# S5 scan: factors and one product of each step held in a PSUM bank

## The chip, the cores and the metric

The kernel runs on one core of a Trainium2 chip. The metric is the device time of one execution in microseconds; the time before is the median of three runs.

## The reference, cut to what matters

The model is a two-layer hybrid: layer 0 mixes an SSD block and an S5 block, layer 1 is attention. 256 context tokens and 2048 latent tokens make 2304 positions. The change lies in the S5 block, whose recurrence is, per group g (32 groups), state p (64 states) and direction (two):

```python
step = jnp.exp(log_step)[:, None]
mag = jnp.exp(lr * step)
ab_re, ab_im = mag * jnp.cos(li * step), mag * jnp.sin(li * step)   # the constant factor, complex
# h[t] = ab * h[t-1] + bu[t], complex, as real and imaginary parts
_, _, h_re, h_im = lax.associative_scan(_complex_affine_combine, (a_re, a_im, bu_re, bu_im), axis=1)
y = einsum('btgp,gip->btgi', h_re, c_re) - einsum('btgp,gip->btgi', h_im, c_im)
```

All of it is float32, and the output is compared in float32.

## The kernel before

The program is one launch that goes through its stages in order: modulation and projections of layer 0, SSD, S5, the output of layer 0 with the projections of layer 1, attention. In the S5 stage (`s5`, from line 1114) a chunk is 16 positions, so there are NK = 144 chunks. Each partition holds one of 64 states of one of two directions (forward on partitions 0 to 63, backward on 64 to 127). V is a tile of 128 x 145 x 2 x 32: chunk, real or imaginary part, group.

The S5 stage has three parts. The first (`front_u`, `front_b`, `chunk_inputs`, up to line 1206) fills V[:, 1:] with what each chunk adds to the state. The second (lines 1305 to 1323) is the scan over chunks, 143 steps, each of four VectorE instructions on 64 columns: line 1308 multiplies the state by the real factor A1 into t0, line 1309 multiplies the state with its two parts exchanged by A2 (the imaginary factor, minus and plus) into t1, line 1310 adds the next chunk's input to t0, and line 1311 adds t1 and writes the new state into V. A1 and A2 are two parts of the tile RT that came in by DMA. The third (`states`, `outputs`, `back`) copies V into tiles H (lines 1336 to 1338) and forms the outputs on TensorE.

The order of the work is written out by hand (`manual_schedule`): each engine runs its instructions in the order in which the code issues them, and waits at an instruction for what it needs from others. The loop of the scan also issues work for the other engines:

- `tables(q)` at steps 0, 16, ..., 112: six GpSimd tensor_tensor instructions on 128 x 1088, through `ctable` (lines 1137 to 1145). They depend on nothing in the scan.
- `tables_mm(q - 1)` at the same steps from 16 on, the last one behind the scan: eight TensorE products (line 1293), four ScalarE evictions (line 1294) and six DMAs to the table E in DRAM.
- `load_tt` (line 1251) and `own_chunk` every seventh step from 39: the part of the output inside a chunk, on TensorE (line 1257) and ScalarE (line 1265), into tile uT.
- every seventh step one step of the late modulation (`modulation`, lines 65 to 117): in this order a VectorE store `col` (line 104) of the job three steps back, a TensorE transpose `modt` (line 99) of the job two steps back, a ScalarE copy `modr` (line 90), and the products of a new job (lines 85 and 86), then the fetch of the weights two jobs ahead on SyncE (lines 78 and 80). `modt` has one buffer, so a transpose waits for the store of the transpose before. Only jobs 4 to 11 have a transpose and a store; the stores come with steps 49, 56, ..., 98.

PSUM in this stage: pool `s5ps` has three tags with two banks each, pool `s5m` one bank for `modt`.

Of the kernel before, what the change touches and what calls it, by code (L numbers as in the profile page):

```python
# [9 lines left out]
F32 = mybir.dt.float32  # L10
# [4 lines left out]
ALU = mybir.AluOpType  # L15
# [4 lines left out]
P = 128  # L20
# [99 lines left out]
def late_modulation(E, pool, wps, bank):  # L120

    return modulation(E, [(0, 2 * DM, 3 * DM, None), (1, 0, 3 * DM, E.col1)], 256, pool, wps, bank=bank)
# [851 lines left out]
NG = 32  # L974
# [47 lines left out]
def s5_views(t, parts=S5R):  # L1022

    R, o = {}, 0
    for n, w in parts:
        f = t[:, o:o + w]
        R[n] = f.rearrange("p (g j) -> p g j", j=16) if n in ("bbr", "bbi", "cr", "nci") else f.rearrange("p (n g) -> p n g", g=NG)
        o += w
    return R
# [84 lines left out]
def s5(E, finish, slots):  # L1114
# [4 lines left out]
    v, gp = nc.vector, nc.gpsimd  # L1119
    with ExitStack() as ctx:  # L1120
        pp = ctx.enter_context(tc.tile_pool(name="s5par", bufs=1, reuse_waits="tile"))
        RT = pp.tile([P, sum(w for _, w in S5R[2:])], F32, tag="RT", name="RT")
        R = s5_views(RT, S5R[2:])
        uT = pp.tile([P, NG, 2, NK], F32, tag="s5uT", name="s5uT")
        V = pp.tile([P, NK + 1, 2, NG], F32, tag="s5V", name="s5V")
        ctx.enter_context(tc.manual_schedule())

        def ctable(pr, pi, xr, xi, n, conj, o_r, o_i, tile_, engines):

            shp = [P, 4, n, 16]
            t, t2 = [tile_(i, shp) for i in range(2)]
            pw = lambda a: a.rearrange("p n g -> p g n").unsqueeze(3).to_broadcast(shp)
            xv = lambda a: a.unsqueeze(2).to_broadcast(shp)
            er, ei, g = engines
            g.tensor_tensor(out=t, in0=pw(pi), in1=xv(xi), op=ALU.mult)
            er.tensor_tensor(out=o_r, in0=pw(pr), in1=xv(xr), op=ALU.mult)
            g.tensor_tensor(out=t2, in0=pw(pi), in1=xv(xr), op=ALU.mult)
            yield  # L1140
            er.tensor_tensor(out=o_r, in0=o_r, in1=t, op=ALU.add if conj else ALU.subtract)
            yield
            ei.tensor_tensor(out=o_i, in0=pw(pr), in1=xv(xi), op=ALU.mult)
            yield
            ei.tensor_tensor(out=o_i, in0=o_i, in1=t2, op=ALU.subtract if conj else ALU.add)
# [100 lines left out]
        def load_tt(g, tt=None):  # L1246
            if tt is None:
                tt = ty.tile([P, 2, 256], F32, tag="tt", name="tt")
            ea = S["E"][g]
            for sb in range(2):  # L1250
                nc.sync.dma_start(out=tt[:, sb], in_=bass.AP(ea.tensor, ea.offset + P * sb, [[16, 8], [ESZ, 16], [1, 256]]))
            TT[g] = tt
# [6 lines left out]
        def own_chunk(g):  # L1259

            py = ps.tile([P, 2, NK], F32, tag="pu", name="py")
            for tb in range(2):
                within(g, py, tb)
            del TT[g]
            nc.scalar.activation(out=uT[:, g], in_=py, func=AF.Copy)
# [5 lines left out]
        with tc.tile_pool(name="s5s", bufs=2, reuse_waits="tile") as ss:  # L1271
            L48 = [ty.tile([P, 4, 48], F32, tag="L" + n, name="L" + n, bufs=1) for n in ("bbr", "bbi")]
            for t in L48:
                gp.memset(t, 0.0)

            def inputs(q):
                for n, t in zip(("bbr", "bbi"), L48):
                    for a, o in ((F, 0), (B, 16), (slice(0, P), 32)):
                        nc.scalar.activation(out=t[a, :, o:o + 16], in_=R[n][a, 4 * q:4 * q + 4], func=AF.Copy)

            def tables(q):
                sl = slice(4 * q, 4 * q + 4)
                for _ in ctable(R["PCr"][:, :, sl], R["PCi"][:, :, sl], R["cr"][:, sl], R["nci"][:, sl], 17, True, *CT[q],
                                lambda i, s: ss.tile(s, F32, tag=f"ct{i}", name="ct", bufs=1), (gp, gp, gp)):
                    pass

            def tables_mm(q):
                for g in (0, 2):
                    Q = ss.tile([48, 2, 272], F32, tag="Q", name="Q", bufs=2)
                    for gl in range(2):  # L1290
                        pq = ps.tile([48, 272], F32, tag="pv", name="pq")
                        for ri in range(2):
                            nc.tensor.matmul(pq, L48[ri][:, g + gl], fl(CT[q][ri][:, g + gl], 0, 17), start=(ri == 0), stop=(ri == 1))
                        nc.scalar.activation(out=Q[:, gl], in_=pq, func=AF.Copy)
                    dst = S["E"][4 * q + g:4 * q + g + 2].rearrange("g j e -> j g e")
                    nc.sync.dma_start(out=dst[:, :, 0:240], in_=Q[0:16, :, 16:256])
                    nc.sync.dma_start(out=dst[:, :, 256:496], in_=Q[16:32, :, 0:240])
                    nc.sync.dma_start(out=dst[:, :, 240:256], in_=Q[32:48, :, 256:272])
                if q < 7:
                    inputs(q + 1)  # L1300

            mps = ctx.enter_context(tc.tile_pool(name="s5m", bufs=2, space=PSUM, reuse_waits="tile"))
            mods = late_modulation(E, ss, mps, lambda: ps.tile([P, 512], F32, tag="pb", name="modps"))
            inputs(0)
            for i in range(NK - 1):
                t0 = ss.tile([P, 2, NG], F32, tag="t0", name="t0")
                t1 = ss.tile([P, 2, NG], F32, tag="t1", name="t1")
                v.tensor_tensor(out=t0, in0=V[:, i], in1=R["A1"], op=ALU.mult)
                v.tensor_tensor(out=t1, in0=V[:, i][:, ::-1], in1=R["A2"], op=ALU.mult)
                v.tensor_tensor(out=t0, in0=t0, in1=V[:, i + 1], op=ALU.add)  # L1310
                v.tensor_tensor(out=V[:, i + 1], in0=t0, in1=t1, op=ALU.add)
                if i % 16 == 0 and i // 16 < 8:
                    tables(i // 16)
                    if i:
                        tables_mm(i // 16 - 1)
                if i + 14 in AHEAD:
                    load_tt(AHEAD[i + 14])
                if i in AHEAD:
                    own_chunk(AHEAD[i])
                if mods and i % 7 == 0:  # L1320
                    mods.pop(0)()
            while mods:
                mods.pop(0)()
            tables_mm(7)
# [90 lines left out]
        for g in range(NG):  # L1415
# [6 lines left out]
            if g >= NG - 8 and g < NG - 4:  # L1422
                i = g % 4
# [770 lines left out]
def tile_hybrid(ctx, tc, I, out, phases=None, preload=None, dumps=None):  # L2194
# [35 lines left out]
    with tc.tile_pool(name="dts", bufs=1, side="right", reuse_waits="tile") as dts:  # L2230
        finish = lambda: None
        if on("A"):
            finish = even_projections(E, dts.tile([P, 512], F32, tag="dt", name="dt"))
        slots = Slots(early.enter_context(tc.tile_pool(name="slots", bufs=1, reuse_waits="tile")))
        if on("S"):
            s5(E, finish, slots)
        else:
            finish()
# [96 lines left out]
```

## Time and profile before

| | us |
|---|---|
| median of 3 runs | 4036.66 (4035.59 to 4037.07) |
| profiled execution | 4034.8 |
| its span, first to last instruction | 4033.1 |
| TensorE busy | 3720.1 (92%) |
| VectorE busy | 2754.4 (68%) |
| GpSimd busy | 2196.0 (54%) |
| ScalarE busy | 1850.9 (46%) |

Rows carry times from the start of the span. PE is TensorE's matmul, PEld its weight load, DVE VectorE, ACT ScalarE, POOL GpSimd, SP SyncE. L1308 is line 1308 of the kernel before. A busy share is an average over all stages; what an edit in one stage is worth is read from the rows of that stage.

### The profile page before, as it was taken

The numbers are of one execution on the slowest core, as the hardware profiler recorded it, in microseconds if no ns is written. First come the engines' busy times: TensorE is split into PE (matmuls) and PEld (weight loads), VectorE is DVE, ScalarE is ACT, GpSimd is POOL, SyncE is SP. The second block draws the span as 40 slices with busy tenths as digits, with TensorE's granted clock in tenths as the row PEclk, the third lists the DMA queues.
The fourth block names the chain that finished last, engine by engine and source line by source line (L and its number), as shares of the span: only waits on it lengthen the run. The fifth ranks groups of instructions, "written<-read, shape, count | busy, mean of one in ns | idle before, by whom it ended". The sixth has DMA issues, their size and how long they took to land.

```text
span 4033.1 us, 72188 instructions
## 1 busy us (share of the span) xinstructions
PE 3720.1 (92%) x27102; PEld 3145.1 (78%) x27102; DVE 2754.4 (68%) x5006; ACT 1850.9 (46%) x3195; POOL 2196.0 (54%) x2120
## 2 busy tenths in 40 slices
PE   7999998638889999999999997899999999999998
PEld 4888886316888888788778886788888888888887
DVE  5366767997687888711455453877777777777775
ACT  4422224203435565411222222666666666666665
POOL 2111113731233999522333332988888888888886
PEclk9999999869999999999999998999999999999999
DMA  7512323324667667533332225889888888888885
GB/s 262 176 56 66 98 69 93 109 66 118 210 221 257 228 235 241 191 123 131 129 110 85 94 79 146 173 143 159 162 157 154 154 153 157 152 151 158 153 163 115
DMA packets 998591, 594.49 MB, mean 147 GB/s; under 512 B 711849, under 2 KB 908249, under 8 KB 996193
## 3 DMA queue, kind: packets, MB, share of 16 engines
q1 hardware_dynamic: 984112, 563.35, 56.2%
q10 hardware_dynamic: 14128, 26.51, 1.8%
q8 instruction: 214, 3.51, 0.3%
q14 instruction: 137, 1.11, 0.1%
HBM read 296.63 MB, written 125.32 MB: 105 GB/s over the span
## 4 chain that ended last, share of the span: by engine, by line
PE 48%; DVE 5%; POOL 3%; issue 1%; DMA 1%; ACT 1%; SPq 0%; DVEq 0%; POOLq 0%; ACTq 0%
PE s L1996 11%; PE mm L43 6%; PE mm L41 6%; PE mm L42 6%; PE tp L2025 5%; PE pv L2054 5%; PE pv L2056 3%; PE po L2111 2%; DVE st L1998 2%; PE po L2112 1%; PE po L2113 1%; POOL nat L2014 1%; DVE lo L2035 1%; POOL nat L2013 1%; DVE ol L35 1%
## 5 line engine op out<-in xcount | busy, mean ns | idle before, releaser
L2006 ACT ACTIVATE st<-st,mx 128x768 f32<-128x768 f32 x768 | 714.5, 930 | 355.5 <-DVE mx L2002 271.8
L2014 POOL TENSOR_TENSOR nat<-st,nat 128x768 f16<-128x768 f32 (+1 forms) x512 | 727.0, 1420 | 42.7
L1996 PE MATMUL s<-KS,q 128*128 128x512 f32 (+1 forms) x3072 | 693.7, 351 | 40.3 <-DVE mx L1998 39.8
L1998 DVE CUSTOM_DVE_ANT_0 st<-s,zero,mx 128x768 f32<-128x768 f32 x512 | 519.3, 1014 | 278.8 <-PE s L1996 203.6
L1996 PEld LDWEIGHTS s<-KS,q 128*128 128x128 f32 x3072 | 536.1, 190 | 136.8 <-DVE mx L1998 47.7
L2013 POOL TENSOR_SCALAR nat<-st 128x768 f16<-128x768 f32 (+1 forms) x512 | 387.6, 757 | 187.4 <-ACT st L2006 187.2
L2025 PE MATMUL tp<-ident,st 128*128 128x128 f32 x2048 | 280.9, 277 | 36.4 <-DVE ol L35 22.3
L2035 DVE TENSOR_TENSOR lo<-tp,hi 128x1024 f16<-128x1024 f32 x256 | 312.3, 1220 | 2.9 <-ACT hi L2030 2.9
L2054 PE MATMUL pv<-V,T 128*128 128x129 f16 x2560 | 310.8, 222 | 2.4 <-DMA T<-nat 2.3
L41 PE MATMUL mmps<-ah,wh 128*128 128x512 f32 (+1 forms) x800 | 304.7, 381 | 3.8 <-DVE ah L214 3.8
L42 PE MATMUL mmps<-al,wh 128*128 128x512 f32 (+1 forms) x800 | 299.1, 374 | 0.3 <-DVE al L35 0.3
L43 PE MATMUL mmps<-ah,wl 128*128 128x512 f32 (+1 forms) x800 | 298.9, 374 | 0.0
L2030 ACT ACTIVATE hi<-tp 128x1024 f16<-128x1024 f32 x256 | 259.2, 1012 | 40.8 <-PE tp L2025 36.0
L2025 PEld LDWEIGHTS tp<-ident,st 128*128 128x128 f32 x2048 | 228.3, 142 | 62.5 <-DVE ol L35 28.4
L1998 DVE CUSTOM_DVE_ANT_0 st<-s,zero 128x768 f32<-128x768 f32 x256 | 243.0, 949 | 44.1 <-POOL nat L2014 26.1
L41 PE MATMUL mm<-w,ah 128*128 128x512 f32 x656 | 263.0, 401 | 1.5 <-ACT ah L1675 1.5
L42 PE MATMUL mm<-w,ah 128*128 128x512 f32 x656 | 257.2, 392 | 1.4 <-DVE w L35 1.4
L43 PE MATMUL mm<-w,al 128*128 128x512 f32 x656 | 257.5, 392 | 0.0
L2056 PE MATMUL pv<-V,T 128*128 128x65 f16 x2560 | 249.7, 193 | 0.0
L277 DVE SCALAR_TENSOR_TENSOR acc<-raw,convw,acc 128x512 f32<-128x512 f32 (+1 forms) x320 | 223.5, 698 | 35.8 <-POOL raw L270 11.8
L2054 PEld LDWEIGHTS <-T 128*128 128x128 f16 x2560 | 234.1, 97 | 14.2 <-DMA T<-nat 3.3
L2054 PE MATMUL pv<-V,hi 128*128 128x129 f16 x2048 | 220.7, 220 | 0.0
(429 smaller groups left out, 9094.4 us busy)
## 6 DMA issues: line engine op xcount, KB each, us to landing
ac<-acs SPq DMA_DIRECT2D x72, 512.0 KB
q<-q SPq DMA_DIRECT2D x128, 256.0 KB
x<-xn SPq DMA_DIRECT2D x35, 512.0 KB
h<-h SPq DMA_DIRECT2D x34, 512.0 KB
x<-in_x_dram SPq DMA_DIRECT2D x32, 512.0 KB
adaw<-in_ada_w_dram SPq DMA_DIRECT2D x32, 512.0 KB
a<-aT SPq DMA_DIRECT2D x32, 512.0 KB
wr<-in_ev_w_dram SPq DMA_DIRECT2D x38, 256.0 KB
```

The source lines that it names most:

```text
L41: nc.tensor.matmul(ps, ah(k), bh(k), start=first and k == 0, stop=False)
L42: nc.tensor.matmul(ps, ah(k), bl(k), start=False, stop=False)
L43: nc.tensor.matmul(ps, al(k), bh(k), start=False, stop=last and k == n - 1)
L1996: nc.tensor.matmul(ps[:, c0:c0 + n], Q[:, hh % 2, i, hh // 2], KS[kv][:, b * TH + c0:b * TH + c0 + n], start=(i == 0), stop=(i == 1))
L1998: v.tensor_tensor_reduce(out=st, in0=ps[:, :TH], in1=zero.to_broadcast([P, TH]), scale=1.0, scalar=NEG if b == 0 else mx[:, b - 1:b], op0= ...
L2006: nc.scalar.activation(out=st, in_=st, func=AF.Exp, bias=UN[u]["mx"][:, 6:7])
L2013: gp.tensor_scalar(out=nat[:, 0], in0=p, scalar1=1.0, scalar2=0.0, op0=ALU.mult, op1=ALU.add)
L2014: gp.tensor_tensor(out=nat[:, 1], in0=p, in1=nat[:, 0], op=ALU.subtract)
L2025: nc.tensor.transpose(pt[:, j], UN[u]["st"][b][:, k * P:(k + 1) * P], E.ident)
L2035: v.tensor_tensor(out=lo, in0=UN[u]["pt"], in1=hi, op=ALU.subtract)
L2054: nc.tensor.matmul(pv[:, 0:129], hi, V2[:, c, kv, 0:129], start=first, stop=end)
L2056: nc.tensor.matmul(pv[:, 0:65], lo, V2[:, c, kv, 0:65], start=False, stop=False)
```

## The change

A PSUM tile X of 128 x 4 x 2 x 32 float32 (1 KB of a partition) is taken from pool `s5m`. Parts 0 and 1 receive copies of A1 and A2 ahead of the loop; parts 2 and 3 serve as t0 in turn. t1, V and everything else stay where they are.

```diff
             mods = late_modulation(E, ss, mps, lambda: ps.tile([P, 512], F32, tag="pb", name="modps"))
             inputs(0)
+
+            X = mps.tile([P, 4, 2, NG], F32, tag="scan", name="scan", bufs=1)
+            for k, n in enumerate(("A1", "A2")):
+                v.tensor_copy(X[:, k], R[n])
             for i in range(NK - 1):
-                t0 = ss.tile([P, 2, NG], F32, tag="t0", name="t0")
+                t0 = X[:, 2 + i % 2]
                 t1 = ss.tile([P, 2, NG], F32, tag="t1", name="t1")
-                v.tensor_tensor(out=t0, in0=V[:, i], in1=R["A1"], op=ALU.mult)
-                v.tensor_tensor(out=t1, in0=V[:, i][:, ::-1], in1=R["A2"], op=ALU.mult)
+                v.tensor_tensor(out=t0, in0=V[:, i], in1=X[:, 0], op=ALU.mult)
+                v.tensor_tensor(out=t1, in0=V[:, i][:, ::-1], in1=X[:, 1], op=ALU.mult)
                 v.tensor_tensor(out=t0, in0=t0, in1=V[:, i + 1], op=ALU.add)
                 v.tensor_tensor(out=V[:, i + 1], in0=t0, in1=t1, op=ALU.add)
```

## Rows read from the trace of the kernel before

**Rows 1.** The page's first part: busy us (share of the span) xinstructions, by engine.

```profile
PE 3720.1 (92%) x27102; PEld 3145.1 (78%) x27102; DVE 2754.4 (68%) x5006; ACT 1850.9 (46%) x3195; POOL 2196.0 (54%) x2120
```

**Rows 2.** Busy times by stage: window, length, PE, PEld, DVE, ACT, POOL, PEclk, DMA, GB/s.

```profile
737.00:839.00 102.00, 41.34 (x188) 16.93 (x186) 101.11 (x53) 12.50 (x43) 101.37 (x47) 0.73 0.27 87
839.00:868.60 29.60, 0.00 (x0) 0.00 (x0) 27.03 (x150) 0.00 (x0) 0.73 (x3) 0.50 0.00 0
868.60:936.40 67.80, 67.47 (x328) 32.79 (x328) 58.87 (x334) 17.48 (x60) 0.00 (x0) 0.98 0.47 152
```

**Rows 3.** Timeline, first stretch: start us, us, engine, line, operation, shapes, [idle before].

```profile
804.97 2.47 POOL L1141 TENSOR_TENSOR ct<-ct 128x1088 f32<-128x1088 f32 x1
805.01 2.51 DVE L1310 TENSOR_TENSOR t<-t,s5V 128x64 f32<-128x64 f32 x1
```

**Rows 4.** Timeline of VectorE, second stretch: one scan step and the next one's start.

```profile
840.18 0.22 DVE L1308 TENSOR_TENSOR t<-s5V,RT 128x64 f32<-128x64 f32 x1
840.32 0.22 DVE L1309 TENSOR_TENSOR t<-s5V,RT 128x64 f32<-128x64 f32 x1
840.45 0.22 DVE L1310 TENSOR_TENSOR t<-t,s5V 128x64 f32<-128x64 f32 x1
840.71 0.22 DVE L1311 TENSOR_TENSOR s5V<-t,t 128x64 f32<-128x64 f32 x1
840.96 0.22 DVE L1308 TENSOR_TENSOR t<-s5V,RT 128x64 f32<-128x64 f32 x1
```

**Rows 5.** Timeline of TensorE's matmuls in the scan.

```profile
777.71 0.62 PE L1293 MATMUL pq<-ct,Lbbi 128*48 128x272 f32 x2
...
868.79 0.37 PE L99 MATMUL modt<-ident,modr 2*128 2x2 f32 x2 [90.45 <-DVE col L104]
869.09 4.92 PE L85 MATMUL modps<-adaw,sc 128*2 128x256 f32 x16
...
875.85 3.62 PE L85 MATMUL modps<-adaw,sc 128*2 128x256 f32 x16
...
910.50 0.28 PE L99 MATMUL modt<-ident,modr 2*128 2x2 f32 x2
```

**Rows 6.** Timeline of VectorE: three stores of the modulation and the scan's last instruction.

```profile
868.57 0.16 DVE L104 TENSOR_SCALAR col<-modt 128x4 f32<-128x4 f32 x1
...
905.37 0.16 DVE L104 TENSOR_SCALAR col<-modt 128x4 f32<-128x4 f32 x1 [3.63 <-PE modt L99]
...
910.85 0.15 DVE L104 TENSOR_SCALAR col<-modt 128x4 f32<-128x4 f32 x1
...
945.41 0.23 DVE L1311 TENSOR_TENSOR s5V<-t,t 128x64 f32<-128x64 f32 x1
```

**Rows 7.** Timeline of ScalarE where the scan ends.

```profile
949.82 0.39 ACT L1294 ACTIVATE Q<-pq 48x272 f32<-48x272 f32 x1 [0.48 <-PE pq L1293]
950.11 3.32 ACT L1336 ACTIVATE H<-s5V 64x576 f32<-64x576 f32 x3
```

**Rows 8.** Timeline of GpSimd: the last instruction of tables 3 and 7.

```profile
782.92 2.48 POOL L1145 TENSOR_TENSOR ct<-ct 128x1088 f32<-128x1088 f32 x1
...
836.33 2.48 POOL L1145 TENSOR_TENSOR ct<-ct 128x1088 f32<-128x1088 f32 x1
```

**Rows 9.** Attention: line 2035 (ns min/median/max, starts), busy times of a window (as rows 2).

```profile
L2035 DVE TENSOR_TENSOR lo<-tp,hi x256: 1216/1219/1225, 2524.5 to 4003.0; 128x1024 f16<-128x1024 f32 x128
...
2800.00:2900.00 100.00, 96.13 (x1033) 85.89 (x1030) 79.51 (x151) 68.20 (x93) 83.85 (x85) 1.00 0.86 157
```

**Rows 10.** VectorE's groups by form: count | busy us, mean ns | idle before.

```profile
L367 DVE TENSOR_TENSOR x<-prep,bias 128x64 f32<-128x64 f32 x8 | 1.4, 218 | 3.7 <-PE prep L365 3.7
...
L1205 DVE COPY s5V<-pv 64x32 f32<-64x32 f32 x32 | 6.9, 217 | 6.8 <-ACT s5V L1204 6.1
...
L1109 DVE COPY RT<-PWi 128x32 f32<-128x32 f32 x1 | 0.2, 172 | 0.0
```

**Rows 11.** Timeline of ScalarE: a copy out of a bank that VectorE reads too.

```profile
960.54 0.37 ACT L1369 ACTIVATE yc<-po 16x256 f32<-16x256 f32 x1 [0.96 <-DVE yl L1368]
```

## The prediction, made before the changed kernel ran

> **What bounds the kernel now.** I read the page first: TensorE is busy for 92% of the span, VectorE 68%, GpSimd 54% [rows 1]. That average is of no use here, because the change sits in one stage, the S5 scan between 737 and 946 us. So next came the busy times of that stretch by stage. From 737 to 839 us VectorE and GpSimd are both busy all the time, but VectorE finishes only 53 instructions in 101.11 us; from 839 to 868.6 it finishes 150 in 27.03 us, and TensorE does nothing at all; from 868.6 to 936.4 TensorE is busy for 67.47 of 67.80 us [rows 2]. The same four instructions thus cost ten times more in the first stretch. The timeline shows why: a scan instruction starts 0.04 us after a GpSimd product of the tables and ends 0.1 us after that product has ended, 2.51 us for 64 columns [rows 3]. Once GpSimd is through, an identical instruction lasts 0.22 us, and a scan step takes 840.96 - 840.18 = 0.78 us [rows 4] (from 840.18 to 846.48 eight steps, 0.7875 each). In the slow stretch one scan instruction goes through for each GpSimd instruction, 52 for 48 (four slip into gaps). So 13 of the 143 steps eat 101.8 us.
>
> Who waits for that? The TensorE timeline has the answer: its last product of the third table ends at 777.71 + 0.62 = 778.3 us, and its next instruction, a transpose for the modulation, starts at 868.79 after 90.45 us idle on VectorE's `col` (line 104) [rows 5]. This store is issued behind scan step 49 and lands at 868.57 + 0.16 [rows 6]. From there TensorE's queue runs without a gap to 936 us, waits a little for `tt`, does the last table, and ScalarE evicts that table until 950.2 and then begins H, the input of the next stage, at 950.11 [rows 7]. The scan itself ends at 945.64, and its last 44 steps follow the store at 910.85 [rows 6]. So the end of this stage is set by TensorE's chain that starts with the store behind step 49; the scan's tail comes in 4.5 us before it. In between VectorE once waited 3.63 us for TensorE [rows 6], which is the sign that after step 49 TensorE is the slower of the two.
>
> **The change part by part.**
> *The reads.* Lines 1308 and 1309 take the factor from PSUM, lines 1310 and 1311 take t0 from PSUM. No scan instruction has two SBUF operands any more. Whether that ends the waiting is to be seen in the attention stage: `lo<-tp,hi`, a VectorE tensor_tensor with one operand in PSUM and one in SBUF, lasts 1216 to 1225 ns in all of its 256 executions, while GpSimd is busy for 83.85 us of 100 with two-operand work [rows 9]. Not one of them stretches. I take the waiting as gone. Then 13 steps cost 13 x 0.7875 = 10.2 us in place of 101.8.
>
> *Price of an operand in PSUM.* Read side: `x<-prep,bias`, 128x64 with one operand in PSUM, 218 ns [rows 10], as the scan's 0.22 us with both in SBUF [rows 4]: no difference. The other bound: a PSUM copy of 32 columns takes 217 ns, an SBUF copy of 32 columns 172 [rows 10], 45 ns more (that one writes with a stride, so it is a high bound). No row has VectorE writing PSUM, which lines 1308 and 1310 now do; I bound it by the same 0 to 45 ns. Nothing in the rows would make an operand in PSUM cheaper than one in SBUF, so below nothing is left out. I take 0, since the row with the same shape and operation says so; with 45 ns on all four instructions a step is 0.7875 + 0.18 = 0.97 us.
>
> [...]
>
> *Order inside the bank.* Factors and both t0 now share one bank. In this program accesses of two engines to one bank are put in order even when both only read: ScalarE's `yc<-po` waits for VectorE's `yl` [rows 11], which reads the same bank. If VectorE's own accesses are ordered by bank too, line 1309 (reads X) must wait for line 1308 (writes X). Today 1309 starts 0.14 us behind 1308, and a true dependent starts 0.255 behind (1310 to 1311) [rows 4]: 0.115 us more per step, 0.90 in all. Behind 1309 on VectorE stand 1310, 1311 and the rest of the scan. No other engine touches the bank. I take no such wait, for reading order on one engine needs none; its price is kept as a rival.
>
> *Two copies* of 64 columns ahead of the scan: at most 2 x 0.22 us, and one of them beside the other: the scan starts at about 737.7 in place of 737.41. This is hidden (next part), since VectorE reaches step 49 before TensorE does. Bank count: the new tile takes the one bank that pools `s5ps` (six) and `s5m` (one) leave free; nothing waits for it, since it is first written behind VectorE's own last read of the stage before.
>
> *GpSimd.* Its 48 instructions come back to back at 2.1 to 2.4 us already; table 3 is done at 785.4 and table 7 at 838.8 [rows 8], before as after.
>
> *The new path.* Step 49 ends at 737.7 + 50 x 0.7875 = 777.1, its store at 777.3. TensorE is free at 778.3: it doesn't wait at all. Its queue moves from 868.79 to 778.35, that is by 90.45 us. Besides, the first modulation product after the long idle took 4.92 us where the next took 3.62 [rows 5] (the granted clock had stood at 0.50 of full speed, [rows 2]): without the idle time 1.3 us more are saved. Sum: 91.7 us. Does something else become late? The fourth table's products stand 16.6 us behind the transpose, so at 793.7 with table 3 ready at 785.4; the last table's at 853.3 with table 7 ready at 838.8: GpSimd is never late. The step-98 store needs the transpose of 910.50 [rows 5], now at 818.8, and VectorE is there by 816.4; 44 further steps bring the scan's end to 853.9. ScalarE's last table eviction moves from 950.2 to 858.5, so H starts at 858.4, 4.5 us behind the scan. The weights of the modulation and the `tt` loads, which SyncE issues from this queue, move along by the same 91 us into a stretch in which today nothing runs on the DMAs, so they meet no new traffic; later stages follow H and shift whole.
>
> **Sum.** The profiled execution took 4034.8 us (span 4033.1 and 1.7 around it), so 4034.8 - 91.7 = 3943.1. The median of the three runs, 4036.66, is 1.9 us above that; 4036.66 - 91.7 = 3945 is the forecast. It has slack: a step may cost up to (778.3 - 737.7) / 50 = 0.81 us with nothing lost.
>
> **Rivals.**
> 1. *Bank order*, step 0.90 us. Step 49 and its store end at 783.0, TensorE's chain shifts by 85.7; the scan ends at 737.7 + 143 x 0.9025 + about 0.7 for eight stores = 867.4, behind ScalarE's 864.5. H moves from 950.1 to 867.4, 82.7 us: 3954. For it: [rows 11]. Against: that is an order between two engines.
> 2. *PSUM dearer*, step 0.97 (45 ns on each instruction): the scan ends at 877.2, gain 73 us, 3964; together with the bank order 1.08, end 893, gain 57, 3980. For it: no row of a PSUM write, and a PSUM write whose result is read next lies twice on the step's chain. Against: 218 ns in [rows 10]. [...]
> 3. *No release*: the conflict comes from the write into SBUF or from any SBUF access beside GpSimd. Then 52 instructions again take 101.8 us and the time stays at 4037. Against: [rows 9], whose output goes to SBUF.
> 4. *Slower*: the trip through PSUM, write and dependent read, is long, and the scan itself becomes the stage. It decides from the step at which the scan ends at 950.1: (950.1 - 738.4) / 143 = 1.48 us, 0.37 per instruction on the average against 0.20 today. With 1.6 us a step the scan ends at 967.2 and the kernel loses 17 us: 4054. Against: the rows show nothing above 45 ns, and this needs some 170.
>
> **How the numbers follow.** Chances: forecast 0.52, bank order 0.20, PSUM dearer 0.18, no release 0.06, slower 0.04. A measurement of this kernel tells about 0.2% (8 us) from no change. All of the first three are faster by over 1%: 0.90; to that I add 0.02 of the no-release case in which only a part of the instructions is released: faster 0.92, same 0.04, slower 0.04. The range reaches from 3939 (forecast less some 6 us: the transfers and the clock may do a little better) to 3978 (PSUM dearer on all four instructions and most of the bank order too).
>
> **What would show it.** Right: scan instructions of 0.21 to 0.23 us from 737 us on, beside GpSimd's 2.1 to 2.5 us; a step of 0.79 us; TensorE's idle before line 99 gone, its queue without a gap from 778 to about 845; the scan's end at about 854 and H at 858. Bank order: 1309 starting 0.25 us behind 1308. PSUM dearer: lines 1308 and 1310 at 0.26 us or more. No release: 2 us instructions beside GpSimd. The forecast falls with a step above 0.85 us, or if TensorE stands idle again at the transpose of line 99 for another reason, such as a table of GpSimd's that comes late.

## The result, and the profile after

The changed kernel takes 3971.7 us (median of 6 runs, 3965.3 to 3975.74) against 4037.62 of the kernel before (6 runs): ratio 0.9834, 95% interval 0.9821 to 0.9847. That is 65.9 us less. The forecast was 91.7 us less, 3945; the time lies inside the range, 27 us above the forecast.

The profiled execution has a span of 3969.7 us, 63.4 less than before. Nearly all of that arises in the S5 stage: ScalarE begins H at 887.08 in place of 950.11 [rows 7], 63.0 us earlier. Lines of the scan have moved: 1308 to 1311 before are 1312 to 1315 now, 1336 is 1340.

First VectorE beside GpSimd, which answers to [rows 3]; this is the timeline (start us, us, engine, line, operation) of the changed kernel:

```profile
801.03 2.14 POOL L1138 TENSOR_TENSOR ct<-RT 128x1088 f32<-128x1088 f32 x1
801.11 0.23 DVE L1314 TENSOR_TENSOR scan<-scan,s5V 128x64 f32<-128x64 f32 x1
801.38 0.22 DVE L1315 TENSOR_TENSOR s5V<-scan,t 128x64 f32<-128x64 f32 x1
801.64 0.23 DVE L1312 TENSOR_TENSOR scan<-s5V,scan 128x64 f32<-128x64 f32 x1
```

The GpSimd product lasts 2.14 us (line 1138 took 2.13 us before), and the three scan instructions shown run beside it unstretched. The waiting is gone. The price of the operands is in the view by line of the changed kernel (ns min/median/max, first and last start):

```profile
L1312 DVE TENSOR_TENSOR scan<-s5V,scan x143: 228/228/230, 738.1 to 886.0; 128x64 f32<-128x64 f32 x143
L1313 DVE TENSOR_TENSOR t<-s5V,scan x143: 220/220/222, 738.3 to 886.3; 128x64 f32<-128x64 f32 x143
L1314 DVE TENSOR_TENSOR scan<-scan,s5V x143: 231/232/233, 738.6 to 886.6; 128x64 f32<-128x64 f32 x143
L1315 DVE TENSOR_TENSOR s5V<-scan,t x143: 224/224/225, 738.9 to 886.8; 128x64 f32<-128x64 f32 x143
```

No execution of 143 is longer than 233 ns; the sum of the four medians, 904 ns, is 19 ns above that of before (224, 218, 218 and 225 ns, together 885). But the starts have moved apart. This is one step and the next one's start, to be held against [rows 4]:

```profile
739.11 0.23 DVE L1312 TENSOR_TENSOR scan<-s5V,scan 128x64 f32<-128x64 f32 x1
739.38 0.22 DVE L1313 TENSOR_TENSOR t<-s5V,scan 128x64 f32<-128x64 f32 x1
739.63 0.23 DVE L1314 TENSOR_TENSOR scan<-scan,s5V 128x64 f32<-128x64 f32 x1
739.90 0.22 DVE L1315 TENSOR_TENSOR s5V<-scan,t 128x64 f32<-128x64 f32 x1
740.15 0.23 DVE L1312 TENSOR_TENSOR scan<-s5V,scan 128x64 f32<-128x64 f32 x1
```

Before, the second started 0.14 us behind the first and the third 0.13 us behind the second; now each of the four starts 0.25 to 0.27 behind the one ahead of it. A step takes 1.04 us in place of 0.7875. In the compiled program of the changed kernel each of the four carries a wait on VectorE's own count for the instruction just ahead; in the program before, the second has none and the third waits only for the first.

What this does to TensorE is seen in its timeline, which answers to [rows 5]:

```profile
777.92 0.62 PE L1293 MATMUL pq<-ct,Lbbi 128*48 128x272 f32 x2
790.27 0.37 PE L99 MATMUL modt<-ident,modr 2*128 2x2 f32 x2 [11.73 <-DVE col L104]
790.57 4.98 PE L85 MATMUL modps<-adaw,sc 128*2 128x256 f32 x16
...
797.65 0.25 PE L99 MATMUL modt<-ident,modr 2*128 2x2 f32 x2 [0.41 <-DVE col L104]
797.84 3.62 PE L85 MATMUL modps<-adaw,sc 128*2 128x256 f32 x16
...
804.95 0.25 PE L99 MATMUL modt<-ident,modr 2*128 2x2 f32 x2 [1.80 <-DVE col L104]
...
834.32 0.28 PE L99 MATMUL modt<-ident,modr 2*128 2x2 f32 x2
```

The store behind step 49 comes at 790 and not at 777, so 11.73 of the 90.45 idle us remain, and the first product behind them again takes 4.98 us. From there on the queue needs 44.05 us to the transpose of 834.32, where it needed 41.71 before (868.79 to 910.50): it waits for the next two stores as well, 0.41 and 1.80 us. And at the end the order has turned round, which the timeline of ScalarE, the counterpart of [rows 7], shows:

```profile
873.89 0.39 ACT L1294 ACTIVATE Q<-pq 48x272 f32<-48x272 f32 x1 [0.48 <-PE pq L1293]
887.08 3.32 ACT L1340 ACTIVATE H<-s5V 64x576 f32<-64x576 f32 x3 [12.80 <-DVE s5V L1315]
```

The last table is evicted by 874.3, and ScalarE then stands idle for 12.80 us until the scan has written its last state. Before, it was the other way round: the scan had ended 4.5 us earlier. The scan itself now sets the end of the stage: 738.07 + 143 x 1.04 = 886.8.

### The profile page after: what moved, and what is told of

It is laid out like the page before. It is cut to its first block, busy times and chain, and to the rows that moved or that the text cites. A ratio compares the mean times of both kernels' runs of the same rounds, so it can differ in the third digit from the quotient of the medians.

```text
span 3969.7 us, 72190 instructions
## 1 busy us (share of the span) xinstructions
PE 3714.5 (94%) x27102; PEld 3137.8 (79%) x27102; DVE 2687.4 (68%) x5008; ACT 1850.2 (47%) x3195; POOL 2191.9 (55%) x2120
## 4 chain that ended last, share of the span: by engine, by line
PE 49%; DVE 5%; POOL 2%; ACT 1%; issue 1%; DMA 1%; DVEq 0%; SPq 0%; POOLq 0%; ACTq 0%
PE s L2000 11%; PE mm L43 6%; PE mm L41 6%; PE mm L42 6%; PE tp L2029 5%; PE pv L2058 5%; PE pv L2060 3%; DVE st L2002 2%; PE po L2115 2%; PE po L2116 1%; PE po L2117 1%; POOL nat L2018 1%; DVE lo L2039 1%; POOL nat L2017 1%; DVE ol L35 1%
## 5 line engine op out<-in xcount | busy, mean ns | idle before, releaser
L2002 DVE CUSTOM_DVE_ANT_0 st<-s,zero 128x768 f32<-128x768 f32 x256 | 242.9, 949 | 43.9 <-POOL nat L2018 26.9
```

The costliest lines, as they stand in the source:

```text
L2002: v.tensor_tensor_reduce(out=st, in0=ps[:, :TH], in1=zero.to_broadcast([P, TH]), scale=1.0, scalar=NEG if b == 0 else mx[:, b - 1:b], op0= ...
```

## The experiments

The question was where 29 of the 92 us had gone. Theory: the program orders the accesses to the one PSUM tile, which takes the overlap out of the step. Rival: an operand in PSUM costs this by itself. Two further runs test the collision with GpSimd operand by operand, and one takes away what GpSimd reads. Then two runs close what the first left open.

**Factors and t0 in two banks.** The changed kernel, with t0 in a tile and a bank of its own. Six banks of `s5ps`, one for `modt` and one for X were in use, and the one for t0 comes from `own_chunk`, which gets a single buffer during the scan.

```diff
-            X = mps.tile([P, 4, 2, NG], F32, tag="scan", name="scan", bufs=1)
+            X = mps.tile([P, 2, 2, NG], F32, tag="scan", name="scan", bufs=1)
+            Y = mps.tile([P, 2, 2, NG], F32, tag="t0", name="t0", bufs=1)
...
-                t0 = X[:, 2 + i % 2]
+                t0 = Y[:, i % 2]
...
-            py = ps.tile([P, 2, NK], F32, tag="pu", name="py")                # own_chunk
+            py = mps.tile([P, 2, NK], F32, tag="pu", name="py", bufs=1)
...
-            mps = ctx.enter_context(tc.tile_pool(name="s5m", ...))
+            scan = ctx.enter_context(ExitStack())
+            mps = scan.enter_context(tc.tile_pool(name="s5m", ...))
...
             tables_mm(7)
+            scan.close()
+        pus = ctx.enter_context(tc.tile_pool(name="s5pu", bufs=2, space=PSUM, reuse_waits="tile"))
...
-            py = ps.tile([P, 2, NK], F32, tag="pu", name="py")                # outputs
+            py = pus.tile([P, 2, NK], F32, tag="pu", name="py")
```

> The factors and the two t0 lie in two PSUM banks instead of one; to have the eighth bank, own_chunk takes one buffer in the scan, and the output stage has a pool of its own. All operands still come from PSUM as in the changed kernel. Theory (order inside the bank: the program makes each of the four instructions wait for the one before because they share a bank): the second instruction starts 0.14 us behind the first again, the third is no longer held by the second, a step is 0.79 to 0.81 us, TensorE's idle before the transpose of step 49 goes from 11.7 us to under 2, and the kernel takes about 3946 us. Rival (an operand in PSUM itself holds the next instruction): the starts stay at 0.26 us, the step at 1.04 and the kernel at about 3972 us.

Measured: 3942.62 us (median of 5), ratio to the kernel before 0.9756, interval 0.9743 to 0.9769, faster than the changed kernel too. The timeline of VectorE, one step and the next one's start:

```profile
739.32 0.23 DVE L1314 TENSOR_TENSOR t<-s5V,scan 128x64 f32<-128x64 f32 x1
739.46 0.21 DVE L1315 TENSOR_TENSOR t<-s5V,scan 128x64 f32<-128x64 f32 x1
739.59 0.23 DVE L1316 TENSOR_TENSOR t<-t,s5V 128x64 f32<-128x64 f32 x1
739.85 0.22 DVE L1317 TENSOR_TENSOR s5V<-t,t 128x64 f32<-128x64 f32 x1
740.11 0.23 DVE L1314 TENSOR_TENSOR t<-s5V,scan 128x64 f32<-128x64 f32 x1
```

A step is 0.79 us, with the same operands in PSUM and the same reads and writes. In the compiled program the second instruction again has no wait, and the third waits only for the first, as in the program before. The rival is out. Every waypoint of the forecast is met; here is TensorE's timeline at step 49, and ScalarE's at H:

```profile
778.25 0.62 PE L1293 MATMUL pq<-ct,Lbbi 128*48 128x272 f32 x2
778.80 0.28 PE L99 MATMUL modt<-ident,modr 2*128 2x2 f32 x2
779.01 3.62 PE L85 MATMUL modps<-adaw,sc 128*2 128x256 f32 x16
```

```profile
858.16 0.39 ACT L1294 ACTIVATE Q<-pq 48x272 f32<-48x272 f32 x1 [0.48 <-PE pq L1293]
858.46 3.32 ACT L1344 ACTIVATE H<-s5V 64x576 f32<-64x576 f32 x3
```

TensorE doesn't wait at the transpose, its first product takes 3.62 us, and H starts at 858.46 (forecast 858.4), right behind the last table, with the scan's last instruction at 853.95 + 0.22 = 854.2 (forecast 853.9). The stage gains 91.6 us. The medians make 98 us of the whole (4040.31 for the kernel before in this series, interval 93 to 104) and the profiled executions 85 (4033.1 - 3948.1). The five executions spread over 10.8 us, from 3939.1 to 3949.86, and the profiled one is the longest; what differs from 91.6 lies in the later stages, and no run here says why.

**Only the factors in PSUM.** The changed kernel, with t0 back in SBUF.

```diff
-            X = mps.tile([P, 4, 2, NG], F32, tag="scan", name="scan", bufs=1)
+            X = mps.tile([P, 2, 2, NG], F32, tag="scan", name="scan", bufs=1)
...
-                t0 = X[:, 2 + i % 2]
+                t0 = ss.tile([P, 2, NG], F32, tag="t0", name="t0")
```

> Only the factors are in PSUM, t0 stays in SBUF: the first two instructions of a step have one SBUF operand, the last two have two. Theory (the number of SBUF operands of the single instruction decides): beside GpSimd's tables the first two take 0.22 us and only the last two are stretched to 2 us, so about 24 steps instead of 13 are done by 839 us; after that, with no write into the bank, a step is 0.79 us; step 49 ends about 9 us earlier than before, kernel about 4028 us. Rival (reading PSUM holds the next instruction): after 839 us a step of 0.9 us or more, kernel 4032 or more.

Measured: 4031.81 us (one execution). VectorE's groups between 738 and 838 us (count | busy us, mean ns | idle before):

```profile
L1314 DVE TENSOR_TENSOR t<-t,s5V 128x64 f32<-128x64 f32 x22 | 45.8, 2080 | 0.0
L1315 DVE TENSOR_TENSOR s5V<-t,t 128x64 f32<-128x64 f32 x22 | 45.3, 2059 | 0.8
L1312 DVE TENSOR_TENSOR t<-s5V,scan 128x64 f32<-128x64 f32 x22 | 4.9, 221 | 0.8
L1313 DVE TENSOR_TENSOR t<-s5V,scan 128x64 f32<-128x64 f32 x22 | 4.7, 214 | 0.0
```

**Only t0 in PSUM.** The kernel before, with t0 taken from a PSUM tile of two parts.

```diff
+            Y = mps.tile([P, 2, 2, NG], F32, tag="t0", name="t0", bufs=1)
             for i in range(NK - 1):
-                t0 = ss.tile([P, 2, NG], F32, tag="t0", name="t0")
+                t0 = Y[:, i % 2]
```

> Only t0 is in PSUM, the factors stay in SBUF. Theory: the first two instructions of a step are stretched to 2 us beside GpSimd's tables, the last two take 0.22 to 0.23 us; after 839 us a step is 0.79 to 0.81 us, since the second instruction doesn't touch the bank; kernel about 4028 us. Rival (a write into PSUM holds the next instruction): after 839 us the second instruction starts 0.25 us behind the first, step 0.9 us or more, kernel 4032 or more.

Measured: 4030.59 us (one execution). The same view:

```profile
L1310 DVE TENSOR_TENSOR t<-s5V,RT 128x64 f32<-128x64 f32 x23 | 48.2, 2095 | 0.0
L1309 DVE TENSOR_TENSOR t<-s5V,RT 128x64 f32<-128x64 f32 x24 | 45.2, 1883 | 0.8
L1312 DVE TENSOR_TENSOR s5V<-t,t 128x64 f32<-128x64 f32 x23 | 5.2, 225 | 0.8
L1311 DVE TENSOR_TENSOR t<-t,s5V 128x64 f32<-128x64 f32 x23 | 5.1, 220 | 0.0
```

The two runs are mirror images: the two instructions with two SBUF operands take 1.9 to 2.1 us on the mean, the two with one take 0.21 to 0.23, in one loop and beside the same GpSimd work. What decides is the single instruction's operands. Some 22 or 23 steps are done by 839 us (24 expected, 13 before), TensorE's wait at step 49 is 82.0 us in both in place of 90.45, and H starts at 942.71 and 942.27, 7.4 and 7.8 us earlier than before. The spans are only 3.0 and 4.2 us below that of before (4030.1 and 4028.9). The expected 9 us are thus nearly met in the stage and missed in the whole; but nine executions of the kernel before in this series spread over 8.8 us (4035.57 to 4044.36), so one execution of each cannot tell 4028 from the rivals' 4032. The steps decide, not the totals. In both, a step after 839 us takes 0.78 to 0.79 us (844.91 to 845.69 and 845.37 to 846.16): neither reading from PSUM nor writing into it holds the next instruction.

**GpSimd writes and doesn't read.** The kernel before, with six fills in place of the six products of each table; the tables, and with them the S5 output, are left out of the computation.

```diff
-                for _ in ctable(R["PCr"][:, :, sl], ..., (gp, gp, gp)):
-                    pass
+                for t in 3 * CT[q]:
+                    gp.memset(t, 0.01)
```

> The kernel before, scan untouched (all operands in SBUF), but GpSimd's six products of each table are replaced by six fills of the same tiles with a constant, which read nothing; the tables of the output stage and what follows from them are thereby not the reference's. Theory (VectorE's second SBUF operand collides with what GpSimd reads): the scan is not stretched, a step is 0.79 us from its start, step 49 ends at about 777 us, and the kernel gains what the forecast said, about 92 us: 3946 us. Rival (any use of SBUF by GpSimd blocks): scan instructions last as long as the fills beside them, about 1 us each.

Measured: 3945.6 us (one execution). The timeline while GpSimd fills:

```profile
740.13 3.85 POOL L1284 MEMSET ct<- 128x1088 f32 x4
740.96 0.22 DVE L1307 TENSOR_TENSOR t<-s5V,RT 128x64 f32<-128x64 f32 x1
741.11 0.22 DVE L1308 TENSOR_TENSOR t<-s5V,RT 128x64 f32<-128x64 f32 x1
741.24 0.22 DVE L1309 TENSOR_TENSOR t<-t,s5V 128x64 f32<-128x64 f32 x1
741.50 0.23 DVE L1310 TENSOR_TENSOR s5V<-t,t 128x64 f32<-128x64 f32 x1
```

Scan instructions with two SBUF operands run unhindered beside GpSimd's writes: the medians of the four lines are 218 to 224 ns, the longest of 572 executions 307 (the fills last until 771.5, some 43 steps), where beside the products one took 2.51 us [rows 3]. So in this kernel the collision is between a second operand in SBUF and what GpSimd reads; a GpSimd instruction with one operand to read was not tried here. The run is at the same time the forecast's arithmetic with nothing in PSUM at all: a step of 0.79 us from the start gives H at 857.43, where the forecast had 858.4. That the total of this one execution lies 0.6 us from the 3945 forecast is chance, given the spread of 8.8 us.

**One tile over two banks.** The first run changed two things at once, the bank and the tile. Here factors and t0 lie in two banks again but are parts of one tile of 4 KB; the pools are those of the first run.

```diff
-            X = mps.tile([P, 4, 2, NG], F32, tag="scan", name="scan", bufs=1)
+            X = mps.tile([P, 2, 4, 2, 64], F32, tag="scan", name="scan", bufs=1).rearrange("p b k r c -> p b k (r c)")
+            Y = X[:, 1].rearrange("p k (r g) -> p k r g", g=NG)[:, :, 0:2]
+            X = X[:, 0].rearrange("p k (r g) -> p k r g", g=NG)[:, :, 0:2]
...
-                t0 = X[:, 2 + i % 2]
+                t0 = Y[:, i % 2]
```

> Pools as in the version with two banks, and factors and t0 again lie in two banks, but both are parts of one PSUM tile of 4 KB. In the compiled program each of the four instructions again waits for the one before it, as in the changed kernel. Theory (what costs is the wait that the program puts between accesses to one PSUM tile, not the bank itself): the second instruction starts 0.26 us behind the first, the step is 1.04 us, the kernel about 3972 us. Rival (the chip is slow where one bank is read and written at the same time): step 0.79 us, kernel about 3944 us.

Measured: 3968.99 us (median of 4), ratio 0.983, interval 0.9813 to 0.9848, like the changed kernel. VectorE's timeline:

```profile
741.88 0.23 DVE L1315 TENSOR_TENSOR scan<-s5V,scan 128x64 f32<-128x64 f32 x1
742.14 0.22 DVE L1316 TENSOR_TENSOR t<-s5V,scan 128x64 f32<-128x64 f32 x1
742.39 0.23 DVE L1317 TENSOR_TENSOR scan<-scan,s5V 128x64 f32<-128x64 f32 x1
742.66 0.22 DVE L1318 TENSOR_TENSOR s5V<-scan,t 128x64 f32<-128x64 f32 x1
742.92 0.23 DVE L1315 TENSOR_TENSOR scan<-s5V,scan 128x64 f32<-128x64 f32 x1
```

1.04 us again, with factors and t0 in different banks; from the run with two banks this one differs only in that they are parts of one tile. So a shared bank is not needed for the loss; the wait that the program puts between two accesses to one PSUM tile is enough. Two tiles in one bank were not tried, so it is not shown whether sharing a bank alone would cost anything.

**The pools alone.** The control for the first run: one tile as in the changed kernel, pools of the first run.

```diff
-            py = ps.tile([P, 2, NK], F32, tag="pu", name="py")                # own_chunk
+            py = mps.tile([P, 2, NK], F32, tag="pu", name="py", bufs=1)
...
             tables_mm(7)
+            scan.close()
...
```

The lines left out are those of the pools in the first run.

> Control for the version with two banks: only its rearranged pools (one buffer for own_chunk in the scan, a pool of its own for the output stage), with factors and t0 in one tile as in the changed kernel. Theory (the gain of the two-bank version comes from the order inside the step alone): step 1.04 us, kernel 3972 us as the changed one, to 5 us. Rival (the pools bring part of it): below 3964 us.

Measured: 3972.52 us (median of 4), ratio 0.9842, interval 0.9826 to 0.9857; step 1.04 us. The pools bring nothing that can be told from the changed kernel's 3971.7. The gain of the first run is the separate tile.

## Why the prediction was right or wrong

- *What bounds the stage*: right. The TensorE queue stood behind the store of step 49, and taking away the waits of scan instructions on GpSimd moved it; the runs with a step of 0.79 us (two banks, and fills in place of products) show the whole chain at the forecast times, 858.46 and 857.43 for H against 858.4.
- *The reads no longer collide*: right. In the two half changes, beside GpSimd's products, a scan instruction with one SBUF operand takes 0.21 to 0.23 us and one with two 1.9 to 2.1 us on the mean; beside the fills, which read nothing, one with two takes 0.22 us as well (medians 218 to 224 ns). One reading of the evidence was off: of GpSimd's 83.85 us in [rows 9] 26.9 are a TENSOR_SCALAR with one tensor operand (line 2013), so "two-operand work" holds for the rest only; the conclusion does not change.
- *Price of an operand in PSUM*: right, for writes too, which no row had shown: 228 and 232 ns with the result in PSUM (4 and 14 more than the same lines took before), and the two-bank step of 0.79 us is that of before. For reads, line 1313, which takes its factor from PSUM and writes to SBUF, needs 220 ns where it needed 218 with both operands in SBUF. That the stride of the copy makes 45 ns a high bound was the author's estimate; no run shows what a stride costs.
- *Order inside the bank*: this is the step that failed: "I take no such wait, for reading order on one engine needs none". That premise was the author's, and no row showed it. The program does put the wait there: line 1313 starts 0.27 us behind 1312, where 1309 started 0.14 behind 1308. The rival made of it carried the wrong price as well: it counted one extra wait per step, the second instruction behind the first, which reads a tile just written (0.115 us). There are two: the third also waits for the second, since it writes the tile that the second reads. With both a step is 1.04 us, and the rival's own sum gives what was measured: scan end at about 887, H 63 us earlier. The evidence named for it [rows 11] concerned two engines and one bank, and there the bank holds a single tile, `po`, so the rows could not tell bank from tile; the runs show one engine and a tile.
- *The range*: it held 3971.7 in part by luck. Its upper end, 3978, was made of operands in PSUM that cost 45 ns each and most of the bank order at 0.115 us a step. The first is 14 ns at most between the medians of these runs, and the second is about 0.25 us a step.
- *Slack*: the forecast named 0.81 us per step as the limit up to which nothing is lost. At 1.04 the loss came in the two places that its bank-order rival had named: TensorE at the transpose of step 49, with 11.73 us of idle time, and the scan's end, which falls behind the last table.
- *GpSimd and the moved transfers*: right. GpSimd's products stay at 2.1 to 2.5 us, the last table is done by 839.2, and no TensorE product of a table waited for GpSimd. TensorE's waits for `tt` come to 4.1 us where they came to 5.7 before.

## What to carry to other kernels

Before a small tensor_tensor chain runs beside GpSimd work, count its SBUF operands: with two, nearly every 64-column instruction here waited out a whole GpSimd product (52 of them took 101.8 us, at 0.22 us each when GpSimd was through), and one operand in PSUM ended that (0.21 to 0.23 us each) at no price that a step shows (0.79 us with two tiles, as before). But place what is only read and what is written in separate PSUM tiles (here they also lay in separate banks): parts of one PSUM tile were ordered against each other even on one engine, and two such waits cost 0.25 us a step here, 29 us of a 92 us gain. When a step is shorter than its instructions' sum (0.7875 against 0.885 us here), the overlap of starts is a term of its own in the prediction.

## What the runs showed of the hardware

A wait of a VectorE instruction for the one just ahead moved its start, counted from the start of that one, from 0.13 or 0.14 us (kernel before) to between 0.25 and 0.27 us (changed kernel), at 64 columns; the durations (0.21 to 0.23 us) hide this. GpSimd's side of the collision cost it nothing that can be seen: the products of lines 1137 and 1138 start 2.08 us apart beside waiting VectorE instructions (800.78 - 798.70 in the kernel before) and 2.09 us apart beside free ones (801.03 - 798.94 in the changed kernel).
